# A decoder layer on one core: narrower merges, sample pieces scaled on ScalarE and spread over more of the program, early products in four banks, an operand read back from memory

## The chip, the cores and the metric

The kernel runs on one core of a Trainium2 chip. The metric is the device time of one execution in microseconds (us). Before the change three runs took 2405.36, 2413.23 and 2403.6 us; the median is 2405.36 us.

The core's engines, as the profile names them: PE multiplies matrices (PEld is its loading of weights), DVE is the vector engine (VectorE), ACT the scalar engine (ScalarE), POOL is GpSimd, which here mostly issues DMAs, SP issues the other DMAs. Each engine executes its own instructions strictly in the order in which they stand in the program; it waits at an instruction until what this needs is ready.

## What is computed

One inference step of one decoder layer, on 512 tokens of a prompt and 8 tokens that continue 8 samples with caches (T = 520 columns together):

```python
h = rmsnorm(x, ln_mix_pre)
aq, ak, av, bq, bk, bv, bz, bb, ba = split(h @ w_in)
# mixer A: 8 heads, three (window, dilation) branches, merged by softmax denominators
parts = [dilated_branch(aq, kk, vv, wnd, dil, rel_bias) for wnd, dil in ((128, 1), (512, 4), (2048, 16))]
att = merge_branches(parts)
# mixer B: gated delta rule, per token, computed in chunks
#   S_t = a_t (I - b_t k_t k_t^T) S_{t-1} + b_t k_t v_t^T,   o_t = S_t^T q_t
dn_out, conv_new, S_new = delta_mixer(bq, bk, bv, bz, bb, ba, ...)
x = x + rmsnorm(concat(att, dn_out) @ w_out, ln_mix_post)
# channel mixer
up = causal_dwconv(rmsnorm(x, ln_ffn_pre) @ w_ffn_in)      # 2048 -> 2 x 5632
x = x + rmsnorm((gelu(gate) * val) @ w_ffn_out, ln_ffn_post)
```

For a sample, attention reads 129 keys and values per branch from a cache in memory (8 samples x 2048 rows x 8 heads x 128), and the delta rule reads and rewrites a state of 8 samples x 8 heads x 128 x 128. The outputs are the new x for prompt and samples and the new caches and states.

## The kernel before

All large products are done in a split form: each fp32 operand is split into a high part (a cast on ACT) and a low part (a subtraction on DVE), and a product is three products, high x high, high x low and low x high. The 520 columns are handled as two halves, A and B, of 260.

**Units.** The input projection is 49 units, numbered idx 0 to 48. A unit is 128 output rows: 16 blocks of weights, three terms, two halves, 96 matmuls of 260 columns on PE (`gemm`, L148). Its weights come in pieces of 512 KB (`raw`, on SP's queue); `hi` is the cast (ACT, L117), `lo` the subtraction (DVE, L118), in five buffers of four blocks each. Each unit's end runs what depends on it. Units 25 to 40 make the keys and values of prompt attention and run the attention of a head when its second one is done (score maxima L883, transposed values L873 and L956, output copies `attm` L897); units 41 to 48 make the gate z. In between PE does the small matmuls of the delta rule.

**Merges.** The delta rule needs the inverse of a triangular 128 x 128 matrix per chunk and head. Blocks of 32 are inverted on DVE, written to memory (XD, XTD) and read back, and `merge(c)` (L525) joins them for each of four chunks c by small fp32 matmuls: five groups of eight (helper `four`, L520), each 128 weight columns by 128 moving columns, with masks m1 and m2 that keep the blocks that are meant. Its four-head results are `ym` tiles. Merges are emitted at idx 13, 14, 18 and 20.

**Sample work.** The work for the eight samples is one chain of Python generators, `samp`: 18 steps for the delta rule (`sample_dn`), 26 for the scores (`sample_scores`), 25 for the values (`sample_values`). Most steps use one piece `pc` of 512 KB (128 partitions x 8 x 128) of state, key cache or value cache, loaded on POOL's queue, four buffers, three pieces ahead (`ahead`). For a state piece, ACT scales eight blocks (L717), and DVE reduces them (L724) and adds the result (L726), twice. For a key piece DVE does eight product sums (L797). For a value piece DVE does eight scaled adds into `rows` (L833). From idx 25 on three steps are taken after each unit (`step(samp, 3)`), placed behind an instruction of that unit (`tc.issue_after`).

**Mid.** `mid A` and `mid B` are the output projection for the halves: 16 m, each 48 matmuls; ACT evicts each m twice (sqm L1050 and xa or xb L1051). `mid A` also steps `samp`, if anything is left of it.

**Channel mixer.** It is computed by a scheme with seven products of half-size operands (A11, A12, A22 and sums S1 to S4), each product 24 matmuls (`product`, L1264) on weights `hl` (cast L1185, subtraction L1186, four buffers). For the first sixteen blocks (EARLY) the products of A11 and A12 are done ahead, in pairs of two blocks: A11 for both, then A12 added in the same two banks ba and bb, each evicted by ACT to `sp` (L1324) and written to PD. Beside them a generator `gb` works out the half B's operands, a step at a time: S1 to S4 need A11 and A12 whole, which `whole` (L1105) forms again from high and low part by DVE adds (L1109). Then come the main products and the down projection (L1470).

A scheduler places the instructions of each engine from dependencies, priorities (`HI`) and the `issue_after` marks; their order is then fixed.

Of the kernel before, what the change touches and what calls it, by code (L numbers as in the profile page):

```python
# [10 lines left out]
F32 = mybir.dt.float32  # L11
# [15 lines left out]
KT = 16  # L27
H = 8
# [14 lines left out]
def trunk(ctx, tc, I, O):  # L43
# [361 lines left out]
    def col_sums(c, o, keep):  # L405

        p = bank()
        for h in range(4):
            PE.transpose(p[:, h * 128:h * 128 + 128], qkc(o + h, c), ident)
        if keep:  # L410
            kn = Pd.tile([128, 4, 128], F32, name="ym", bufs=3)
            V.tensor_copy(kn.rearrange("p a b -> p (a b)"), p)
            B.dma_start(KND[c], kn)
        jk = Pd.tile([128, 128], F32, name="jk", bufs=2)
        for h in range(4):
            S.activation(jk, p[:, h * 128:h * 128 + 128], AF.Square, accum_out=ss2[:, o // 4, c, h:h + 1])
# [39 lines left out]
    def kk(c, o):  # L456
        p = bank()
        for h in range(4):
            PE.matmul(p[:, h * 128:h * 128 + 128], qkc(4 + h, c), qkc(o + h, c), start=True, stop=True)
        k = Pd.tile([128, 4, 128], F32, name="ym", bufs=3)  # L460
        for h in range(4):
            S.activation(k[:, h, :], p[:, h * 128:h * 128 + 128], AF.Identity, scale=rqk[:, 1, c, h:h + 1])
        return k
# [53 lines left out]
    def four(lhs, rhs, g):  # L517
        p = bank()
        for j in range(4):
            PE.matmul(p[:, j * 128:j * 128 + 128], lhs(4 * g + j), rhs(4 * g + j), start=True, stop=True)  # L520
        return fl(p)

    TT = {}

    def merge(c):  # L525
        N = b4()
        B.dma_start(N, ALD[:, c])
        Tn = b4()
        B.dma_start(Tn, XD[:, c])
        Tt = b4()  # L530
        B.dma_start(Tt, XTD[:, c])
        ym = []
        for g in range(2):
            p = four(lambda h: N[:, h], lambda h: Tn[:, h], g)
            y = Pd.tile([128, 4, 128], F32, name="ym", bufs=3)
            V.tensor_mul(y, p, m1)
            ym.append(y)
        for g in range(2):
            p = four(lambda h: Tt[:, h], lambda h: ym[g][:, h % 4], g)
            pt = four(lambda h: ym[g][:, h % 4], lambda h: Tt[:, h], g)  # L540
            V.tensor_add(Tn[:, 4 * g:4 * g + 4], Tn[:, 4 * g:4 * g + 4], p)
            V.tensor_add(Tt[:, 4 * g:4 * g + 4], Tt[:, 4 * g:4 * g + 4], pt)
        ym = []
        for g in range(2):
            p = four(lambda h: N[:, h], lambda h: Tn[:, h], g)
            y = Pd.tile([128, 4, 128], F32, name="ym", bufs=3)
            V.tensor_mul(y, p, m2)
            ym.append(y)
        for g in range(2):
            pt = four(lambda h: ym[g][:, h % 4], lambda h: Tt[:, h], g)  # L550
            V.tensor_add(Tt[:, 4 * g:4 * g + 4], Tt[:, 4 * g:4 * g + 4], pt)
        TT[c] = Tt

    def scan(c):
# [99 lines left out]
    def ahead(loads):  # L654

        q = []
        for n in range(len(loads)):
            while loads and len(q) <= PCA:
                q.append(loads.pop(0)())
            yield n, q.pop(0)  # L660
# [7 lines left out]
    def sample_dn():  # L668
# [46 lines left out]
        def scaled(dst, src, j, pc):  # L715
            for k in range(8):
                S.activation(dst[:, k], src(k), AF.Identity, scale=kqd[:, j, pc * 8 + k:pc * 8 + k + 1])  # L717

        for pc, sp in ahead([lambda pc=pc: state_piece(pc) for pc in range(8)]):
            for j in range(2):  # L720
                pr = Psm.tile([128, 8, 128], F32, name="prod", bufs=1)
                scaled(pr, lambda k: sp[:, k], j, pc)
                dst = tmp[:, j] if pc else part[:, j * 128:j * 128 + 128]
                V.tensor_reduce(dst, pr.rearrange("p k v -> p v k"), axis=AX.X, op=OP.add)  # L724
                if pc:
                    V.tensor_add(part[:, j * 128:j * 128 + 128], part[:, j * 128:j * 128 + 128], dst)  # L726
            yield
        p = bank("bankX")
        PE.matmul(p[:, 0:258], kon[:, K_PR:K_PR + 128], part, start=True, stop=True)
        na = Psm.tile([128, 2], F32, name="dna")  # L730
# [93 lines left out]
    def sample_values():  # L824
        sc, sbias, stat = SA["sc"], SA["sbias"], SA["stat"]
        rows = Psm.tile([128, H, 128], F32, name="qrep")
        for x, t in ahead([lambda br=br, i=i: cache_piece(I["cache_v"], br, i) for br in range(3) for i in range(8)]):
            for h in range(H):
                w = sc[:, h, x:x + 1]
                if x == 0:  # L830
                    V.tensor_scalar(rows[:, h], t[:, h], w, None, op0=OP.mult)
                else:
                    V.scalar_tensor_tensor(rows[:, h], t[:, h], w, rows[:, h], op0=OP.mult, op1=OP.add)  # L833
            yield
        acc = Psm.tile([128, H, 8], F32, name="sacc")
        p = bank("bankX")
        for h in range(H):
            PE.matmul(p[:, h * 8:h * 8 + 8], rows[:, h], sel8[:, h], start=True, stop=True)
        V.tensor_copy(acc, hb(p[:, 0:64]))
        while len(kvT) < H or len(kvT[H - 1]) < 2:  # L840
            yield

        rows_of(kns, O["s_win_k"])
        rows_of(vns, O["s_win_v"])
        mc, lc, t, e = (stat[:, j] for j in range(4))
        V.tensor_mul(t, qs, kns)
        p = over_partitions(t.rearrange("p a b -> p (a b)"))
        V.tensor_sub(t, sbias[:, :, 24:25].to_broadcast([128, H, 8]), hb(p[:, 0:64]))
        V.tensor_max(e, mc, t)
        V.tensor_sub(t, t, e)  # L850
        V.tensor_sub(e, mc, e)
        S.activation(stat[:, 2:4], stat[:, 2:4], AF.Exp)

        V.tensor_scalar(t, t, 16.0, None, op0=OP.mult)
        V.tensor_mul(acc, acc, e)
        V.tensor_mul(e, lc, e)
        V.tensor_add(e, e, t)
        V.tensor_mul(t, vns, t)
        V.tensor_add(acc, acc, t)
        V.reciprocal(e, e)  # L860
        V.tensor_mul(attm[:, :, 512:520], acc, e)
        yield
# [62 lines left out]
    def step(g, n):  # L925
        for _ in range(n):
            if next(g, "end") == "end":
                return
# [7 lines left out]
    for idx, m in enumerate(mt_order):  # L936
# [50 lines left out]
            inverse()  # L987
        if 10 <= idx < 10 + H:
            bias_rows(idx - 10)
        if idx == 13:  # L990
            merge(0)
        if idx == 14:
            merge(1)
        if idx == 16:
            sample_conv()
# [11 lines left out]
        if idx >= 25:  # L1007

            with tc.issue_after(ev.ins):
                step(samp, 3)  # L1010
    Prs.close()


# [14 lines left out]
                split(MX[k][part], attm[:, k, o:o + w] if k < 8 else vdn[:, k - 8, o:o + w], o, w)  # L1028

    X1D = dram.tile([128, KT, T], F32, name="X1D")  # L1030

    def mid(part, also):

# [25 lines left out]
    def mid2(part, acc, mxs, wk):  # L1059
# [29 lines left out]
        if part == "A":  # L1089
            for g in range(8):  # L1090
                h = scale(g)
                for j in range(2):
                    t = xsA.tile([128, 2, w], F32R, name="xa")
                    split(t, h[:, j], 0, w)
                    XC["A11" if g < 4 else "A12"][2 * (g % 4) + j] = t
                yield
            return
# [4 lines left out]
                split(t, src[:, j], 0, w)  # L1102
                XC[name][2 * i + j] = t

        def whole(name, i):  # L1105
            a = wk.tile([128, 2, w], F32, name="ah", bufs=2)
            for j in range(2):
                t = XC[name][2 * i + j].bitcast(F32)
                V.tensor_add(a[:, j], t[:, 0], t[:, 1])  # L1109
            return a  # L1110

        for i in range(4):
            h1, h2 = scale(i), scale(4 + i)
            put("A22", i, h2, xsB)
            s = wk.tile([128, 2, w], F32, name="sd", bufs=2)
            V.tensor_sub(s, h1, h2)
            yield
            a1, a2 = whole("A11", i), whole("A12", i)
            V.tensor_sub(h1, a1, h1)
            put("S3", i, h1, sxp)  # L1120
            put("S1", i, s, xsB)
            yield
            V.tensor_sub(s, s, a1)
            put("S2", i, s, sxp)
            V.tensor_add(a2, a2, s)
            put("S4", i, a2, sxp)
            yield
# [8 lines left out]

    XC = {n: [None] * 8 for n in ("A11", "A12", "A22", "S1", "S2", "S3", "S4")}
    mix_split("A", mxA)
    a_ = mid("A", lambda m, ev: step(samp, 2))
    run_all(samp)  # L1140
    Pls.close()
    Pmb = ExitStack()
# [172 lines left out]


    for f in range(0, EARLY, 2):
        pp = [fbank(("ba", "bb")[i]) for i in range(2)]
        for k, n in enumerate(("A11", "A12")):
            for i in range(2):  # L1320
                product(pp[i], XC[n], first=k == 0)
                with HI():
                    t = wk2.tile([128, NA], F32, name="sp", bufs=2)
                    S.copy(t, pp[i][:, :NA])  # L1324
                    Q.dma_start(PD[order[f + i]][:, k], t)
                step(gb, 1)
# [326 lines left out]
```

## Time and profile before

| | before |
|---|---|
| median of three runs | 2405.36 us |
| the profiled execution | 2409.24 us |
| its span | 2407.4 us |
| instructions | 47633 |
| DMA traffic | 560.40 MB, mean 233 GB/s |
| PE waits for bankP, bankT and bankS of attention (L895, L873, L880) | 9.3, 6.5 and 3.6 us |
| PE waits for bankX (L1264) behind v L1367 | 6.0 us |
| PE waits for XD (L520) | 5.8 us |
| PE waits for sp in bb (L1264) | 5.3 us |

How to read the rows. A row of the waits names the engine that stood still, what its instruction works on and its line, then behind the arrow the engine and line that ended the wait; then us in all, how often, the longest. A row of the timeline has the start in us from the span's start, the length, engine, line, operation, what is written and read, the shapes, a count of merged instructions, and in brackets the idle time before it and what ended it. In a matmul's shape the first pair is the weights (rows * columns), the second what moves (partitions x columns). An fp32 matmul of the merges stands in the trace as two records. Ends of matmuls overlap, so that the distance between starts is the price of one. A row of the windows has the stretch, its length, the busy time of PE, PEld, DVE, ACT and POOL with counts, the granted clock of PE as a share of full speed, the share of the DMA engines' time and GB/s.

### The profile page before, as it was taken

What the parts mean: (1) busy time and instruction counts of PE and PEld (TensorE: products, weight loads), DVE (VectorE), ACT (ScalarE), POOL (GpSimd) and SP (SyncE); (2) the same over time, 40 slices, a digit from 0 to 9 for tenths busy, and PEclk for the clock granted to TensorE, in tenths of its full rate; (3) what the DMA queues carried; (4) which work ended last, traced back from release to release, by engine and by line L of the source; (5) the groups of instructions that cost most, each with busy time, mean ns of one, the idle gap of its engine ahead of it and who ended that gap; (6) DMA issues with size and microseconds to landing.
All of it is one profiled execution on the core that took longest, in us unless ns stands there. A gap on an engine that the chain in (4) does not pass through costs nothing.

```text
span 2407.4 us, 47633 instructions
## 1 busy us (share of the span) xinstructions
PE 2330.9 (97%) x19046; PEld 2306.0 (96%) x19046; DVE 1743.2 (72%) x3351; ACT 1088.6 (45%) x2124; POOL 173.9 (7%) x275
## 2 busy tenths in 40 slices
PE   8999999998899999899999999999999999999996
PEld 7999999997899999899999999999999999999996
DVE  7789454675789566887888777777777777856348
ACT  6443144683334555553334444444444454533234
POOL 1310110211110000000000000000000000000000
PEclk9999999998999999999999999999999999999998
DMA  5685742558995578878998888888889887687434
GB/s 182 237 288 186 260 158 97 173 176 232 235 197 168 190 246 279 287 226 252 279 274 252 253 262 266 266 260 262 266 264 300 285 313 262 230 297 253 151 112 135
DMA packets 155613, 560.40 MB, mean 233 GB/s; under 512 B 23304, under 2 KB 54968, under 8 KB 153344
## 3 DMA queue, kind: packets, MB, share of 16 engines
q1 hardware_dynamic: 125520, 466.31, 57.8%
q0 software_dynamic: 29872, 91.06, 15.1%
q8 instruction: 149, 2.44, 0.4%
q14 instruction: 72, 0.59, 0.1%
HBM read 498.37 MB, written 195.68 MB: 288 GB/s over the span
## 4 chain that ended last, share of the span: by engine, by line
PE 80%; DVE 7%; DMA 6%; issue 3%; ACT 3%; POOL 1%; SPq 0%; POOLq 0%; DVEq 0%; ACTq 0%
PE ps L1470 21%; PE ps L148 19%; PE bc L1264 10%; PE ba L1264 9%; PE bb L1264 7%; PE bankX L1264 5%; PE bd L1264 5%; DMA pc<-in_cache_k_dram 2%; ACT prod L717 2%; DVE dtmp L724 1%; DVE lo L118 1%; DVE b L502 1%; PE bankX L520 1%; PE bankP L520 1%; DMA XTD<-b 1%
## 5 line engine op out<-in xcount | busy, mean ns | idle before, releaser
L1470 PE MATMUL ps<-xb,hl 128*128 128x260 f32 x2112 | 487.3, 284 | 2.5 <-DVE yacc L1477 2.4
L1470 PE MATMUL ps<-xa,hl 128*128 128x260 f32 x2112 | 485.6, 283 | 0.3 <-DVE yacc L1477 0.2
L148 PE MATMUL ps<-xb,hi 128*128 128x260 f32 x1792 | 462.1, 289 | 0.6 <-ACT hi L117 0.6
L148 PE MATMUL ps<-xa,hi 128*128 128x260 f32 x1792 | 462.1, 289 | 0.3 <-DVE cv L346 0.3
L1470 PEld LDWEIGHTS ps<-xb,hl 128*128 128x128 f32 x2112 | 385.5, 189 | 3.3 <-ACT hl L1185 1.9
L1470 PEld LDWEIGHTS ps<-xa,hl 128*128 128x128 f32 x2112 | 385.6, 189 | 1.2 <-issue 0.7
L148 PEld LDWEIGHTS ps<-xb,hi 128*128 128x128 f32 x1792 | 332.7, 191 | 5.4 <-issue 2.8
L148 PEld LDWEIGHTS ps<-xa,hi 128*128 128x128 f32 x1792 | 333.3, 191 | 3.7 <-issue 1.7
L117 ACT CAST hi<-raw 128x512 fp32r<-128x512 f32 x320 | 194.5, 619 | 280.5 <-PE ps L148 240.8
L118 DVE TENSOR_TENSOR lo<-raw,hi 128x512 fp32r<-128x512 f32 x320 | 217.8, 688 | 116.4 <-ACT hi L117 115.3
L148 PE MATMUL ps<-xb,lo 128*128 128x260 f32 x896 | 258.4, 288 | 1.9 <-DVE lo L118 1.9
L148 PE MATMUL ps<-xa,lo 128*128 128x260 f32 x896 | 257.4, 287 | 0.2 <-DVE lo L118 0.2
L1264 PE MATMUL ba<-xa,hl 128*128 128x260 f32 x1728 | 221.0, 284 | 2.3 <-ACT hl L1185 2.3
L1264 PEld LDWEIGHTS ba<-xa,hl 128*128 128x128 f32 x1728 | 214.0, 190 | 2.4 <-ACT hl L1185 2.4
L1185 ACT CAST hl<-rw 128x1024 fp32r<-128x1024 f32 x131 | 137.6, 1051 | 167.7 <-PE ps L1470 53.9
L1186 DVE TENSOR_TENSOR hl<-rw,hl 128x1024 fp32r<-128x1024 f32 x131 | 160.2, 1223 | 69.0 <-ACT hl L1185 68.0
L1186 DVE TENSOR_TENSOR hl<-rx,hl 128x1024 fp32r<-128x1024 f32 x115 | 140.6, 1223 | 58.3 <-ACT hl L1185 57.9
L148 PEld LDWEIGHTS ps<-xb,lo 128*128 128x128 f32 x896 | 170.3, 190 | 4.3 <-DVE lo L118 2.7
L1185 ACT CAST hl<-rx 128x1024 fp32r<-128x1024 f32 x115 | 120.9, 1052 | 116.2 <-PE ps L1470 68.8
L148 PEld LDWEIGHTS ps<-xa,lo 128*128 128x128 f32 x896 | 170.8, 191 | 1.6 <-issue 0.7
L1185 ACT CAST hl<-rz 128x1024 fp32r<-128x1024 f32 x93 | 97.8, 1052 | 151.3 <-DVE rz L1223 51.3
L1186 DVE TENSOR_TENSOR hl<-rz,hl 128x1024 fp32r<-128x1024 f32 x93 | 113.8, 1224 | 64.2 <-ACT hl L1185 63.7
(579 smaller groups left out, 4193.0 us busy)
## 6 DMA issues: line engine op xcount, KB each, us to landing
raw<-in_w_in_dram SPq DMA_DIRECT2D x98, 512.0 KB, 4.8
raw<-in_w_out_dram SPq DMA_DIRECT2D x64, 512.0 KB, 4.2
rx<-in_w_ffn_in_dram SPq DMA_DIRECT2D x55, 512.0 KB, 6.9
rw<-in_w_ffn_in_dram SPq DMA_DIRECT2D x55, 512.0 KB, 6.1
ry<-in_w_ffn_in_dram SPq DMA_DIRECT2D x49, 512.0 KB, 4.4
rz<-in_w_ffn_in_dram SPq DMA_DIRECT2D x49, 512.0 KB, 6.2
rw<-in_w_ffn_in_dram POOLq DMA_DIRECT2D x44, 512.0 KB, 5.6
UD<-U SPq DMA_DIRECT2D x36, 522.0 KB, 7.2
```

Of the source, the lines that this page charges most:

```text
L117: S.copy(hi, r)
L118: V.tensor_sub(lo, r, hi.bitcast(F32))
L148: PE.matmul(ps[:, PO + o:PO + o + w_], w, X[k][part][:, b, :], start=(i == 0 and j == 0), stop=(i == n - 1 and j == 2))
L502: V.tensor_mul(v, Lb[:, None, 0:i, i].to_broadcast([128, i, i]), X[:, 0:i, 0:i].rearrange("p j m -> p m j"))
L520: PE.matmul(p[:, j * 128:j * 128 + 128], lhs(4 * g + j), rhs(4 * g + j), start=True, stop=True)
L717: S.activation(dst[:, k], src(k), AF.Identity, scale=kqd[:, j, pc * 8 + k:pc * 8 + k + 1])
L724: V.tensor_reduce(dst, pr.rearrange("p k v -> p v k"), axis=AX.X, op=OP.add)
L1185: S.copy(t[:, 0], raw)
L1186: V.tensor_sub(t[:, 1], raw, t[:, 0].bitcast(F32))
L1264: PE.matmul(p[:, 0:NA], w[:, a, k, :], X[k][:, c, :], start=first and n == 0, stop=n == 23, skip_group_check=not first)
L1470: PE.matmul(ps[:, PO + o_:PO + o_ + w_], t[:, a, i * 4 + k, :], act[4 * p + k][part][:, b, :], start=n == 0, stop=n == last)
```

## The change

1. Merges. The products move 64 columns instead of 128: only those halves of the blocks that the masks keep. Where the result has rows that are not needed, the weights are cut to 96 or 64 columns. The middle result of the first half lies in two new tiles YZ of 96 columns, zeroed once at the start. `ym` has two buffers instead of three. Merges of chunks 0 and 1 are emitted a unit later.
2. State pieces. The reduction over eight blocks is replaced by two adds of 512 elements per partition into `sums`, and one reduction at the end for each j.
3. Value pieces. The eight scaled adds on DVE become eight scalings in place on ACT (L848 of the new kernel) and one DVE add of 1024 elements per partition.
4. Two steps of `samp` after each unit instead of three; so 48 of the 69 are taken in the units and the rest in mid A, there two after each m, placed behind the eviction (`after(ev, samp, 2)`).
5. A11 and A12 are written to memory (HD) in fp32 when they are made, 8 tiles of 260 KB, and `whole` reads them back instead of adding the parts.
6. The early products of a pair use banks ba and bb or bc and bd in turn.

```diff
+    YZ = [Pd.tile([128, 4, 96], F32, name="yz", bufs=2) for g in range(2)]
+    for t in YZ:
+        G.memset(t, 0.0)
+
     def merge(c):
...
+        def half(lhs, rhs, g, w, M=128):
+            p = bank()[:M, 0:256].rearrange("p (a b n) -> p a b n", a=4, n=w)
+            for j in range(4):
+                PE.matmul(p[:, j], lhs(4 * g + j), rhs(4 * g + j), start=True, stop=True)
+            return p
...
+        for g in range(2):
+            p = half(lambda h: N[:, h], lambda h: left(Tn)[:, h], g, 32)
+            V.tensor_mul(yl(YZ[g]), p, left(m1))
+        for g in range(2):
+            p = half(lambda h: Tt[:, h], lambda h: yl(YZ[g])[:, h % 4], g, 32)
+            pt = half(lambda h: YZ[g][:, h % 4], lambda h: right(Tt)[:, h], g, 32, 96)
+            V.tensor_add(left(Tn[:, 4 * g:4 * g + 4]), left(Tn[:, 4 * g:4 * g + 4]), p)
+            V.tensor_add(right(Tt[:96, 4 * g:4 * g + 4]), right(Tt[:96, 4 * g:4 * g + 4]), pt)
...
         for pc, sp in ahead([lambda pc=pc: state_piece(pc) for pc in range(8)]):
             for j in range(2):
                 pr = Psm.tile([128, 8, 128], F32, name="prod", bufs=1)
                 scaled(pr, lambda k: sp[:, k], j, pc)
-                dst = tmp[:, j] if pc else part[:, j * 128:j * 128 + 128]
-                V.tensor_reduce(dst, pr.rearrange("p k v -> p v k"), axis=AX.X, op=OP.add)
                 if pc:
-                    V.tensor_add(part[:, j * 128:j * 128 + 128], part[:, j * 128:j * 128 + 128], dst)
+                    V.tensor_add(pr[:, 0:4], pr[:, 0:4], pr[:, 4:8])
+                    V.tensor_add(sums[:, j], sums[:, j], pr[:, 0:4])
+                else:
+                    V.tensor_add(sums[:, j], pr[:, 0:4], pr[:, 4:8])
             yield
+        for j in range(2):
+            V.tensor_reduce(part[:, j * 128:j * 128 + 128], sums[:, j].rearrange("p k v -> p v k"), axis=AX.X, op=OP.add)
...
         for x, t in ahead([lambda br=br, i=i: cache_piece(I["cache_v"], br, i) for br in range(3) for i in range(8)]):
             for h in range(H):
-                w = sc[:, h, x:x + 1]
-                if x == 0:
-                    V.tensor_scalar(rows[:, h], t[:, h], w, None, op0=OP.mult)
-                else:
-                    V.scalar_tensor_tensor(rows[:, h], t[:, h], w, rows[:, h], op0=OP.mult, op1=OP.add)
+                S.activation((t if x else rows)[:, h], t[:, h], AF.Identity, scale=sc[:, h, x:x + 1])
+            if x:
+                V.tensor_add(rows, rows, t)
             yield
...
-        if idx == 13:
+        if idx == 14:
             merge(0)
-        if idx == 14:
+        if idx == 15:
             merge(1)
...
             with tc.issue_after(ev.ins):
-                step(samp, 3)
+                step(samp, 2)
...
             for g in range(8):
                 h = scale(g)
+                Q.dma_start(HD[:, 2 * g:2 * g + 2], h)
...
-        def whole(name, i):
+        def whole(g):
             a = wk.tile([128, 2, w], F32, name="ah", bufs=2)
-            for j in range(2):
-                t = XC[name][2 * i + j].bitcast(F32)
-                V.tensor_add(a[:, j], t[:, 0], t[:, 1])
+            Q.dma_start(a, HD[:, 2 * g:2 * g + 2])
             return a
...
         for i in range(4):
+            a1, a2 = whole(i), whole(4 + i)
             h1, h2 = scale(i), scale(4 + i)
...
-            a1, a2 = whole("A11", i), whole("A12", i)
...
-    a_ = mid("A", lambda m, ev: step(samp, 2))
+    a_ = mid("A", lambda m, ev: after(ev, samp, 2))
...
-        pp = [fbank(("ba", "bb")[i]) for i in range(2)]
+        pp = [fbank((("ba", "bb"), ("bc", "bd"))[f // 2 % 2][i]) for i in range(2)]
```

More of the change, by code (lines that the diff above doesn't have):

```diff
@@ L410, in col_sums @@
         if keep:
-            kn = Pd.tile([128, 4, 128], F32, name="ym", bufs=3)
+            kn = Pd.tile([128, 4, 128], F32, name="ym", bufs=2)
             V.tensor_copy(kn.rearrange("p a b -> p (a b)"), p)
@@ L459, in kk @@
             PE.matmul(p[:, h * 128:h * 128 + 128], qkc(4 + h, c), qkc(o + h, c), start=True, stop=True)
-        k = Pd.tile([128, 4, 128], F32, name="ym", bufs=3)
+        k = Pd.tile([128, 4, 128], F32, name="ym", bufs=2)
         for h in range(4):
@@ L531, in merge @@
         B.dma_start(Tt, XTD[:, c])
+        def half(lhs, rhs, g, w, M=128):
[3 more added lines that the diff above has]
+            return p
+        v = lambda t, w: t.rearrange("p a (b n) -> p a b n", n=w)
+        left, right = (lambda t: v(t, 64)[:, :, :, 0:32]), (lambda t: v(t, 64)[:, :, :, 32:64])
+        yl = lambda t: v(t, 32)[:, :, 0:3:2]
@@ L532, in merge @@
         ym = []
         for g in range(2):
-            p = four(lambda h: N[:, h], lambda h: Tn[:, h], g)
-            y = Pd.tile([128, 4, 128], F32, name="ym", bufs=3)
-            V.tensor_mul(y, p, m1)
+            p = half(lambda h: N[:, h], lambda h: Tn[:, h, None, 0:64], g, 64)
+            y = Pd.tile([128, 4, 128], F32, name="ym", bufs=2)
+            V.tensor_mul(y[:, :, None, 0:64], p, m2[:, :, None, 0:64])
             ym.append(y)
         for g in range(2):
-            p = four(lambda h: Tt[:, h], lambda h: ym[g][:, h % 4], g)
@@ L540, in merge @@
[L540 to L551, printed above, removed]
+            pt = half(lambda h: ym[g][:, h % 4, 0:64], lambda h: Tt[:, h, None, 64:128], g, 64, 64)
@@ L552, in merge @@
+            V.tensor_add(Tt[:64, 4 * g:4 * g + 4, None, 64:128], Tt[:64, 4 * g:4 * g + 4, None, 64:128], pt)
         TT[c] = Tt
@@ L717, in scaled @@
                 S.activation(dst[:, k], src(k), AF.Identity, scale=kqd[:, j, pc * 8 + k:pc * 8 + k + 1])
+        sums = Psm.tile([128, H, 128], F32, name="qrep").rearrange("p (a b) v -> p a b v", a=2)
         for pc, sp in ahead([lambda pc=pc: state_piece(pc) for pc in range(8)]):
@@ L1030, in trunk @@
     X1D = dram.tile([128, KT, T], F32, name="X1D")
+    HD = dram.tile([128, KT, NA], F32, name="HD")
     def mid(part, also):
```

## Prediction

> **What bounds the kernel now.** I read the page first, for the engine that carries the time, then the waits of that engine, then the stretches in which those waits lie.
>
> ```profile
> PE 2330.9 (97%) x19046; PEld 2306.0 (96%) x19046; DVE 1743.2 (72%) x3351; ACT 1088.6 (45%) x2124; POOL 173.9 (7%) x275
> ...
> PE 80%; DVE 7%; DMA 6%; issue 3%; ACT 3%; POOL 1%; SPq 0%; POOLq 0%; DVEq 0%; ACTq 0%
> ```
>
> PE is busy 97% of the span and holds 80% of the chain that ended last. So the kernel gets faster only by fewer or shorter matmuls, or by PE waiting less; work taken from DVE or ACT is worth something only where PE waits for it. Who PE waited for, in us, times, longest:
>
> ```profile
> PE bankP L895 <- DVE attm L897: 9.3, 4, 6.6
> ...
> PE bankT L873 <- DVE vT L956: 6.5, 2, 4.2
> PE bankX L1264 <- DVE v L1367: 6.0, 1, 6.0
> PE bankS L520 <- DMA b<-XD: 5.8, 1, 5.8
> PE bb L1264 <- ACT sp L1324: 5.3, 3, 1.9
> PE bankS L880 <- DVE m L883: 3.6, 2, 3.4
> ```
>
> Three of the six (bankP L895, bankT L873, bankS L880) are one story: prompt attention waits for a DVE that stands elsewhere. The stretches show where, and two later ones beside them (columns: length, busy PE, PEld, DVE, ACT, POOL, granted clock, DMA share, GB/s):
>
> ```profile
> 560.00:580.00 20.00, 11.40 (x71) 11.04 (x70) 10.88 (x61) 4.48 (x9) 3.31 (x6) 0.73 0.74 200
> 580.00:600.00 20.00, 17.73 (x120) 17.02 (x119) 11.85 (x88) 4.44 (x11) 3.13 (x6) 0.85 1.05 229
> 600.00:620.00 20.00, 16.63 (x122) 15.39 (x122) 14.24 (x103) 7.21 (x16) 3.47 (x6) 0.91 0.92 201
> 620.00:640.00 20.00, 15.81 (x115) 15.17 (x115) 15.93 (x122) 4.92 (x12) 3.20 (x6) 0.91 0.94 283
> ...
> 980.00:1000.00 20.00, 14.68 (x115) 14.06 (x115) 15.06 (x18) 10.28 (x18) 0.00 (x0) 0.98 1.02 344
> ...
> 1020.00:1040.00 20.00, 20.00 (x170) 20.00 (x169) 20.00 (x39) 13.68 (x30) 0.00 (x0) 1.00 0.69 211
> ```
>
> From 560 to 640 PE loses 8.6+2.3+3.4+4.2 = 18.4 us of 80 idle, and works at a lower clock besides. These 80 us are the one large hole in the kernel.
>
> **The change part by part.** I sum against the profiled execution, 2409.24 us; the median of the runs, 2405.36, is 3.9 us below it, and I take those 3.9 off at the end.
>
> *Narrow merges.* Each of four merges has five groups of eight products, each product two records on PE: 80 records. All now move 64 columns, not 128. What a record costs is in these PE rows (start, length, line, shapes); weights are the first shape, moving columns the second:
>
> ```profile
> 271.34 0.42 PE L148 MATMUL ps<-xa,lo 128*128 128x260 f32 x1
> 271.56 0.42 PE L148 MATMUL ps<-xb,lo 128*128 128x260 f32 x1
> ...
> 273.01 0.28 PE L148 MATMUL ps<-xb,hi 128*128 128x260 f32 x1
> 273.12 0.28 PE L148 MATMUL ps<-xa,lo 128*128 128x260 f32 x1
> ...
> 273.73 1.05 PE L520 MATMUL bankP<-ym,b 128*128 128x128 f32 x8
> 274.62 1.06 PE L520 MATMUL bankX<-b,ym 128*128 128x128 f32 x8
> ...
> 754.36 0.51 PE L838 MATMUL bankX<-kon,qrep 128*128 128x8 f32 x4
> 754.72 0.36 PE L148 MATMUL ps<-xa,lo 128*128 128x260 f32 x1
> ...
> 961.36 0.60 PE L182 MATMUL bankT<-ones,acc 128*65 128x1 f32 x8 [1.09 <-DVE acc L1055]
> ```
>
> Eight records with 128 moving columns take 274.62 − 273.73 = 0.89 us, 0.111 each. Four with 8 moving columns take 754.72 − 754.36 = 0.36 us, 0.09 each, although they move a sixteenth. Eight with 65 weight columns and one moving column take 0.60 us in all, at most 0.075 each. So a small record follows its weight columns, not its moving ones. Of the 80 new records 48 keep 128 weight columns and save nothing to 0.02 us each; I take nothing, since the 0.09 includes a change from another shape. Sixteen have 96 weight columns and sixteen 64: scaled from 0.111, 0.083 and 0.056, a saving of 16 × 0.028 + 16 × 0.055 = 1.3 us for a merge, **5 us** for four (bounds 0 and, with 0.02 on the 48 as well, 9).
>
> The Trainium skill, "TensorE: Matmul & The Clock Gate", section "Back-to-back issue gap", gives an isolated matmul a gap that grows with its moving columns (N/2.4 + 2.5 ns). By that rule all 320 records would about halve; the row with 8 moving columns disagrees, and it decides.
>
> Emitting two merges one unit later does not touch PE's 5.8 us for XD. The first merge products stand in the same unit as before and wait for the same chain, inverse, write, read; I cost it at nothing. The first row of the change in PE's order (weight columns x moving columns):
>
> ```order
> L148 MATMUL ps<-xa,hi 128x260
> L542 MATMUL bankS<-b_2717,b_2715 128x64 x4
> L542 MATMUL bankT<-b_2717,b_2715 128x64 x4
> L148 MATMUL ps<-xb,hi 128x260
> L148 MATMUL ps<-xa,hi 128x260
> ```
>
> What moved here is only the second number, 128 to 64.
>
> *Two steps per unit.* The hole is the score stage of the samples. DVE needs the cache pieces pc there, and stands in order, with attention's copies behind (tile rows: first and last start at the end):
>
> ```profile
> DVE sjk L797 <- DMA pc<-in_cache_k_dram: 32.2, 12, 9.5
> ...
> L897 DVE COPY attm<-bankP x32: 275/284/295, 435.1 to 696.2; 128x128 f32<-128x128 f32 x32
> ...
> L797 DVE CUSTOM_DVE_ANT_0 sjk<-pc,qrep x192: 269/286/294, 564.1 to 651.4; 128x128 f32<-128x128 f32 x192
> ...
> L779 POOL DMA_DIRECT2D pc<-in_cache_k_dram x16: 578/578/612, 556.5 to 616.4; - x16
> ```
>
> The first piece comes late (a wait of 9.5 us), and 24 pieces then pass in 651.4 − 564.1 = 87 us, 3.7 each: that is the supply. The 32 attm copies belong to eight heads of two units, so a unit with its attention lasts about 261/15 = 17 us. At three pieces a unit the demand is 5.8 us a piece, and a lag of 10 us is made up at 2.1 a piece, over five pieces and more with each new delay. At two a unit the demand is 8.7, and the lag is gone after two. So the first stall stays (6.6 us, the longest for attm) and the others go.
>
> A stall costs more than itself: after the 5.8 us for XD matmuls start 0.22 us apart (271.34, 271.56), two microseconds later 0.11 to 0.12 (273.01, 273.12). In the four stretches the missing clock is 20 × (0.27+0.15+0.09+0.09) = 12 us, part of it in idle time where it costs nothing; I take 9. The hole is then 18.4 + 9 = 27 us, its first stall 6.6 + 2.4 = 9, the gain **18 us** (bounds 10, if two more stalls stay, and 22).
>
> The Trainium skill, same page, section "What's actually happening", lowers the clock after an idle window of about 3.4 us. By that rule the shorter stalls would cost only themselves and the gain would be about 14; the stretch 580:600, idle for 2.3 us in all, shows 0.85, so the trace does not agree.
>
> *Values on ScalarE, in mid A.* With two steps a unit 48 of 69 are done at the end of the units. Four value pieces fall in the last two units and twenty in mid A, two for each of its first ten m. What stands on ACT there (start, length, idle and releaser):
>
> ```profile
> 780.56 0.38 ACT L1050 ACTIVATE sqm<-ps 128x260 f32<-128x260 f32 x1
> 780.84 0.47 ACT L1051 ACTIVATE xa<-ps,cols 128x260 f32<-128x260 f32 x1
> 781.31 0.62 ACT L117 CAST hi<-raw 128x512 fp32r<-128x512 f32 x1
> 783.83 0.62 ACT L117 CAST hi<-raw 128x512 fp32r<-128x512 f32 x1 [1.90 <-PE ps L148]
> 785.27 1.14 ACT L117 CAST hi<-raw 128x512 fp32r<-128x512 f32 x2 [0.82 <-PE ps L148]
> 786.31 0.38 ACT L1050 ACTIVATE sqm<-ps 128x260 f32<-128x260 f32 x1
> ...
> 451.45 2.46 ACT L717 ACTIVATE prod<-pc,dkqd 128x128 f32<-128x128 f32 x8 [1.60 <-DVE dpart L724]
> ```
>
> One m lasts 786.31 − 780.56 = 5.75 us on PE, and ACT works 0.75 for sqm and xa plus four casts at 0.52: 2.85 us. The new operations are those of L717, eight in 2.36 (451.45 to the next at 453.81), 0.295 each; sixteen are 4.7 us. ACT's order in mid A, before (sqm and xa evict one m, hi are the weights of a later one):
>
> ```order
> L117 CAST hi<-raw 128x512 x2
> L1050 ACTIVATE sqm<-ps 128x260
> L1051 ACTIVATE xa<-ps,cols 128x260
> L117 CAST hi<-raw 128x512 x4
> L1050 ACTIVATE sqm<-ps 128x260
> ```
>
> and now:
>
> ```order
> L117 CAST hi<-raw 128x512 x3
> L1068 ACTIVATE sqm<-ps 128x260
> L1069 ACTIVATE xa<-ps,cols 128x260
> L848 ACTIVATE pc<-pc,sc 128x128 x16
> L117 CAST hi<-raw 128x512 x4
> L1068 ACTIVATE sqm<-ps 128x260
> ```
>
> The sixteen stand ahead of the casts that feed PE. 2.85 + 4.7 = 7.55 us against 5.75: ACT becomes the bound for ten m, 75.5 against 57.5 us. Casts run about one m ahead, which hides some 3.5 us: 14.5 us lost.
>
> The pieces must arrive too. In the value stage of before pieces (q0) and weights (q1) together fill the DMA engines from 695 to 715:
>
> ```profile
> DMA packets 1591, 3.96 MB, mean 198 GB/s; under 512 B 629, under 2 KB 629, under 8 KB 1590
> ...
> q0 software_dynamic: 1116, 2.21, 58.6%
> q1 hardware_dynamic: 474, 1.72, 45.8%
> ```
>
> One m needs 1.05 MB of pieces and 1.05 MB of weights, at 198 GB/s 10.6 us. That holds for the first sixteen pieces (two branches); of them seven are used or loaded when mid A begins, and nine are left, 48 us at 5.3 each, while ACT alone would want the ninth 41 us in (five m and half a sixth). So 6.5 us more, 21 in all; I take **20 us** (bounds 14, if transfers keep up, and 40, below). On DVE one add per piece replaces eight operations; DVE is not waited for there, so nothing.
>
> *State pieces by halves.* Shorter DVE work in a stage where PE hardly waits: nothing. *Early products.* PE waits 5.3 us for sp in bb. Four banks remove that, with the clock behind it up to 7 us. But PE's order, before:
>
> ```order
> L1264 MATMUL bb<-xa,hl 128x260 x7
> L190 MATMUL bankP<-nr_y,ones 128x65 x4
> L1264 MATMUL bb<-xa,hl 128x260 x17
> L1264 MATMUL ba<-xa,hl 128x260 x24
> L1264 MATMUL bb<-xa,hl 128x260 x24
> ```
>
> and now:
>
> ```order
> L1281 MATMUL bc<-xa,hl 128x260 x24
> L1281 MATMUL bd<-xa,hl 128x260 x8
> L1281 MATMUL ba<-xa,hl 128x260 x11
> L190 MATMUL bankP<-nr_y,ones 128x65 x4
> L1281 MATMUL ba<-xa,hl 128x260 x13
> L1281 MATMUL bb<-xa,hl 128x260 x24
> L1281 MATMUL bd<-xa,hl 128x260 x16
> ```
>
> starts products of the next pair early and leaves them open. Each holds its hl buffer (four) until its 24 are done, so casts and, behind them on ACT, evictions wait in turn. I take **3 us** gained (bounds 7 gained, 5 lost).
>
> *Operand read back.* Sixteen adds go from DVE, 8 × 260 KB are written and read on SP:
>
> ```profile
> L1109 DVE TENSOR_TENSOR ah<-xa 128x260 f32<-128x260 f32 x16 | 6.0, 424 | 0.0
> ```
>
> DVE is full from 1020 to 1040 yet PE loses nothing there, so the adds were covered; 4.2 MB more cost 0 to 6 us if the 980 to 1000 stretch (share 1.02) lasted for all of it. On SP the reads stand between weight loads, which they hold up if their buffer is late. I take nothing.
>
> Sum: −5 − 18 + 20 − 3 = −6; 2409.2 − 6 = 2403, less 3.9: **2399 us**. The uncovered 6.0 us before L1367 stay, as nothing there changes.
>
> **The rivals.**
>
> (1) ACT has more slack than I gave it and the four banks work: mid A costs 14, early products gain 7. −5 − 18 + 14 − 7 = −16, 2389 us. For it: the 1.90 and 0.82 us that ACT waits for PE in each m; against: the 198 GB/s above.
>
> (2) Slower: the transfers of mid A are the bound. By the share of the rows above one m takes 0.586 × 20 × 1.05/2.21 = 5.6 us of all engines for its pieces and 0.458 × 20 × 1.05/1.72 = 5.6 for its weights, 11.2. If no piece is ahead when mid A starts, six m at 11.2 and four at 7.55 take 97 instead of 57.5, +40. −5 − 18 + 40 − 3 = +14, 2419 us. It turns the whole slower from a loss of 26 us in mid A. For it: the share over 1 at 695 to 715; against: the first seven pieces come in units that last twice an m.
>
> (3) The score stage keeps its stalls, gain 10: −5 − 10 + 20 − 3 = +2, 2407 us. For it: the late first piece is untouched.
>
> (4) Merges pay by moving columns: 320 × 0.111/2 = 18 instead of 5, 2386 us. Against: the row at 754.36. (This is the rule of the Trainium skill's page on TensorE, above.)
>
> **How the numbers follow.** Chances: the forecast 0.42 (2392 to 2407), (1) 0.30, (2) 0.15, (3) 0.07, (4) 0.06. A measurement of this kernel tells about 0.5%, 12 us, from no change: 2393 and 2417. Faster: (4) 0.06, 0.24 of (1), 0.07 of the forecast's low end, 0.37. Slower: 0.12 of (2), 0.02 of the others' high ends, 0.14. The rest, 0.49, is the same. For 8 in 10 the range goes from 2380, which holds (1) and (4) with the bounds of the merges, to 2420, where most of (2) is left out.
>
> **What would show it.** In the profile after: records with 128 weight columns and 64 moving still 0.11 us apart; one PE stall of some 6 us at the first score piece and then none; in mid A an m of 7.5 to 10.6 us, PE idle for hi with ACT busy or waiting for pc; no wait for sp in bb, and some for hl. I am wrong if PE runs through mid A at 5.75 us an m, if the scores keep three or more stalls, or if new waits of over 5 us stand in the early products.

## The result

The changed kernel is slower: 2426.53 us (median of 4 runs, 2420.69 to 2429.43) against 2405.3, ratio 1.0074, 95% interval 1.0058 to 1.0089 (the ratios on record are not quite those of the medians). The forecast was 2399 and the range ended at 2420. The profiled execution has a span of 2427.6 us against 2407.4, 20.2 us more. The time of before differs by a few us from chip to chip (medians 2405 to 2411), so each ratio is taken against the runs of before that were made beside it.

PE does the same work and waits elsewhere. From the page of the changed kernel:

```profile
PE 2335.4 (96%) x19046; PEld 2307.4 (95%) x19046; DVE 1695.0 (70%) x3168; ACT 1140.7 (47%) x2316; POOL 172.7 (7%) x277
...
raw<-in_w_out_dram SPq DMA_DIRECT2D x64, 512.0 KB, 5.6
```

The last row, of the page of before:

```profile
raw<-in_w_out_dram SPq DMA_DIRECT2D x64, 512.0 KB, 4.2
```

Whom PE waited for in the changed kernel:

```profile
PE ps L148 <- ACT hi L117: 15.7, 11, 2.6
PE bankS L542 <- DMA b<-XD: 8.8, 1, 8.8
...
PE ps L148 <- DVE lo L118: 7.9, 12, 0.9
PE bankP L912 <- DVE attm L914: 7.4, 1, 7.4
...
PE ps L148 <- ACT mxA L168: 3.2, 1, 3.2
```

The waits for attention's copies fell from 9.3 + 6.5 + 3.6 us to one of 7.4 (and one of 1.5 for vT); waits for hi, lo and mxA, which were 0.6, 2.1 and 0.4 us, came in. Where that is: I number the large matmuls (260 columns) in PE's order, which both kernels execute in equal number, and subtract the start of the n-th in before from its start in the other trace. Negative is ahead of before. The first unit has 64 of them, so the units end at n = 4672 and mid A at 5440, where the lag is as at 5376; an m is 48. Each lag comes from one trace.

| up to here | n | changed kernel, us | in this part |
|---|---|---|---|
| delta rule with its merges done | 2592 | +1.5 | +1.5 |
| before the first scores | 3456 | −1.2 | −2.7 |
| scores and values of the units | 4512 | −19.2 | −18.0 |
| entry into mid A and mid A | 5376 | +18.6 | +37.8 |
| mid B | 6048 | +17.7 | −0.9 |
| early products | 6912 | +17.1 | −0.6 |
| all the rest | 17823 | +20.2 | +3.1 |

Two parts carry the result. The score stage gained what was forecast; that it is so to the microsecond is luck, as four of the runs below, whose edits only come behind this part, gained 15.6 to 17.3. The same four stretches as in the prediction, now:

```profile
560.00:580.00 20.00, 12.59 (x92) 12.41 (x91) 6.48 (x33) 4.48 (x10) 2.37 (x4) 0.83 0.84 232
580.00:600.00 20.00, 18.43 (x142) 17.11 (x141) 12.98 (x80) 8.68 (x21) 2.91 (x5) 1.00 1.02 232
600.00:620.00 20.00, 20.00 (x170) 19.95 (x169) 13.21 (x82) 6.48 (x14) 2.04 (x4) 1.00 0.79 201
620.00:640.00 20.00, 20.00 (x163) 19.25 (x162) 10.25 (x50) 7.77 (x17) 1.42 (x3) 1.00 0.74 165
```

One stall of 7.4 us is left in the first stretch and one of 1.5 in the second; from 600 on PE is full at full clock. Mid A took it all back, and as much again. ACT there (start, length; idle and what ended it in brackets):

```profile
776.13 0.62 ACT L117 CAST hi<-raw 128x512 fp32r<-128x512 f32 x1 [2.97 <-DMA raw<-in_w_out_dram]
776.65 0.38 ACT L1068 ACTIVATE sqm<-ps 128x260 f32<-128x260 f32 x1
776.93 0.47 ACT L1069 ACTIVATE xa<-ps,cols 128x260 f32<-128x260 f32 x1
777.29 4.79 ACT L848 ACTIVATE pc<-pc,sc 128x128 f32<-128x128 f32 x16
781.97 1.65 ACT L117 CAST hi<-raw 128x512 fp32r<-128x512 f32 x3
787.39 0.62 ACT L117 CAST hi<-raw 128x512 fp32r<-128x512 f32 x1 [3.76 <-DMA raw<-in_w_out_dram]
787.92 0.38 ACT L1068 ACTIVATE sqm<-ps 128x260 f32<-128x260 f32 x1
```

The sixteen scalings stand ahead of the casts and take 4.7 us (777.29 to 781.97), as forecast. But this m lasts 787.92 − 776.65 = 11.3 us instead of 7.55, and what ACT waits for is not a value piece, it is a weight (raw). In the whole of mid A ACT waits for no piece and 10.5 us for weights, and the median weight of the output projection lands 5.6 us after its issue instead of 4.2.

### The profile page after: what moved, and what is told of

It is laid out like the page before. It is cut to its first block, busy times and chain, and to the rows that moved or that the text cites. A ratio compares the mean times of both kernels' runs of the same rounds, so it can differ in the third digit from the quotient of the medians.

```text
span 2427.6 us, 47672 instructions
## 1 busy us (share of the span) xinstructions
PE 2335.4 (96%) x19046; PEld 2307.4 (95%) x19046; DVE 1695.0 (70%) x3168; ACT 1140.7 (47%) x2316; POOL 172.7 (7%) x277
## 4 chain that ended last, share of the span: by engine, by line
PE 60%; DMA 3%; ACT 2%; DVE 2%; issue 1%; SPq 0%; DVEq 0%; ACTq 0%
PE ps L1487 20%; PE bc L1281 11%; PE ba L1281 8%; PE bd L1281 6%; PE bb L1281 6%; PE bankX L1281 5%; PE ps L148 4%; DMA raw<-in_w_out_dram 2%; ACT pc L848 1%; DVE lo L118 1%; ACT hi L117 0%; DVE hl L1203 0%; ACT hl L1202 0%; DMA xb<-ACT 0%; DVE yacc L1541 0%
## 5 line engine op out<-in xcount | busy, mean ns | idle before, releaser
L148 PE MATMUL ps<-xa,hi 128*128 128x260 f32 x1792 | 468.1, 292 | 14.6 <-ACT hi L117 14.3
L1281 PE MATMUL ba<-xa,hl 128*128 128x260 f32 x1536 | 198.7, 286 | 4.4 <-ACT hl L1202 2.3
L1281 PEld LDWEIGHTS ba<-xa,hl 128*128 128x128 f32 x1536 | 191.7, 191 | 5.1 <-ACT sp L1341 2.5
```

The lines of the kernel that those rows point to most:

```text
L148: PE.matmul(ps[:, PO + o:PO + o + w_], w, X[k][part][:, b, :], start=(i == 0 and j == 0), stop=(i == n - 1 and j == 2))
L1281: PE.matmul(p[:, 0:NA], w[:, a, k, :], X[k][:, c, :], start=first and n == 0, stop=n == 23, skip_group_check=not first)
```

## The experiments

The theories: ACT, whose scalings hold up the casts; the transfers, which make weights late; ACT's order alone, with late weights as its consequence. The first two runs take one away each. Lags are those of the table above: mid A is the change of the lag from n = 4512 to 5376.

**The scalings without the loads.**

```diff
-        for x, t in ahead([lambda br=br, i=i: cache_piece(I["cache_v"], br, i) for br in range(3) for i in range(8)]):
+        for x, t in ahead([lambda br=br, i=i: kept(br, i) for br in range(3) for i in range(8)]):
```

(`kept` loads the first eight pieces and then hands out the last four tiles again.)

> The changed kernel, but value pieces 9 to 24 are not loaded: the scalings of mid A and the adds stay and work on the four tiles that pieces 5 to 8 left (so the values of the samples are wrong). ACT's order in mid A stays. In the trace of the changed kernel the stretch from the last units to the end of mid A's sample work loses 38 us against before. Theory 1, ACT is the bound (scalings ahead of the casts, 7.55 us an m): the loss falls to 15, about 2404 us. Theory 2, it is the transfers, and the scalings alone would be hidden by casts that run ahead: the loss falls to 5 or less, about 2392 us. Theory 3, ACT's order does all of it and late weights only follow from it: the loss stays over 30, about 2425 us.

Measured: 2414.54 us in one run, mid A −18.5 to +4.2, a loss of 22.7: no theory's number, above the 15 of the first and below the 30 of the third, while the second, with 5, falls. Between the starts of successive sqm, nine m in a row last 7.4 to 7.6 us, which is the prediction's 7.55 for an m bound by ACT.

**The loads without the scalings.**

```diff
-            for h in range(H):
+            for h in range(H) if x < 4 else ():
                 S.activation((t if x else rows)[:, h], t[:, h], AF.Identity, scale=sc[:, h, x:x + 1])
```

> The changed kernel, but only the first four value pieces are scaled on ACT: the other twenty are loaded and added as they are (so the values of the samples are wrong), and no scaling stands on ACT in mid A. Theory 1 (ACT's 7.55 us an m and late loads add up): the loss of 38 us falls to about 15 to 20, about 2407 us. Theory 2 (transfers): it stays at 30 or more, about 2422 us or over. Theory 3 (ACT's order alone): it falls to 5 or less, about 2392 us.

Measured: 2417.92 us in one run, mid A −15.2 to +6.0, a loss of 21.2. The third theory falls: with no scaling on ACT the weights are late all the same. Mid A from 740 to 860 in before, in the changed kernel, in the run without loads and in the run without scalings (one fence each; the same columns as above), and ACT's wait for weights in that stretch, which before does not have:

```profile
740.00:860.00 120.00, 117.39 (x946) 115.79 (x946) 78.86 (x175) 62.42 (x134) 1.74 (x3) 0.97 0.51 167
```

```profile
740.00:860.00 120.00, 94.87 (x642) 90.20 (x641) 71.49 (x110) 92.00 (x265) 11.83 (x21) 0.86 0.78 202
...
ACT hi L117 <- DMA raw<-in_w_out_dram: 10.5, 6, 3.8
```

```profile
740.00:860.00 120.00, 102.82 (x764) 97.69 (x763) 82.21 (x137) 101.99 (x292) 2.90 (x5) 0.94 0.52 154
...
ACT hi L117 <- DMA raw<-in_w_out_dram: 1.3, 1, 1.3
```

```profile
740.00:860.00 120.00, 103.60 (x776) 100.11 (x775) 83.54 (x143) 59.31 (x138) 11.83 (x21) 0.93 0.83 228
...
ACT hi L117 <- DMA raw<-in_w_out_dram: 32.2, 10, 5.4
```

Without the loads ACT is busy 102 of 120 us and weights are in time but for 1.3 us. Without the scalings ACT is half idle, waits 32.2 us for weights, and PE, busy 103.6 us, is no better off than without the loads (102.8). Either cause alone costs about the same, and together less than their sum, which leaves the question what both runs share.

**Neither.** The last two edits together; only the adds on DVE stay.

> The changed kernel with both taken away: pieces 9 to 24 not loaded and pieces 5 to 24 not scaled, only their adds on DVE stay (so the values of the samples are wrong). With the scalings alone mid A lost 23 us, with the transfers alone 21, with both 38. Theory, two separate causes that overlap: with neither the loss is under 5 us, about 2389 us. Rival, a third cause common to all three runs (the adds on DVE, or the entry into mid A): 10 us or more stay, 2397 us.

Measured: 2397.57 us in one run, mid A −18.7 to −9.8, a loss of 8.9. Between theory and rival, nearer to the rival. Of it 6.3 fall up to n = 4896, that is in the last unit and the first four to five m; I call this the entry. There PE waits, as in the changed kernel, 3.2 us for mxA, whose casts stand on ACT behind the gate of the last unit and the scalings of the units' last pieces, and 3.0 for a cast whose weight came late (the first eight pieces are still loaded in this run, and the first four scaled, so the entry is not free of either cause):

```profile
PE ps L148 <- ACT mxA L168: 3.2, 1, 3.2
PE ps L148 <- ACT hi L117: 3.0, 1, 3.0
PE ps L148 <- DVE mxA L169: 1.4, 2, 0.7
PE ps L148 <- DVE lo L118: 1.1, 2, 0.9
```

Behind the entry, and up to the end of the chain, an m lasts 5.8 us as before, so the adds on DVE, the rival's other cause, cost nothing there. So the 37.8 us are 8.9 for the entry and the rest, 13.8 more for the scalings alone (22.7 − 8.9), 12.3 more for the loads alone (21.2 − 8.9), and 2.8 for both at once. Each figure is a difference of single traces; the 15.6 to 17.3 above show how far such figures scatter, so the 2.8 is not told from nothing.

**Values on DVE, same place.**

```diff
-                S.activation((t if x else rows)[:, h], t[:, h], AF.Identity, scale=sc[:, h, x:x + 1])
-            if x:
-                V.tensor_add(rows, rows, t)
+                w = sc[:, h, x:x + 1]
+                if x == 0:
+                    V.tensor_scalar(rows[:, h], t[:, h], w, None, op0=OP.mult)
+                else:
+                    V.scalar_tensor_tensor(rows[:, h], t[:, h], w, rows[:, h], op0=OP.mult, op1=OP.add)
```

> The changed kernel with the value pieces scaled and added on DVE as before (sixteen operations of 0.29 us in an m, beside four subtractions at 0.58: about 7.1 us a m of 5.75), still two a m in mid A. Theory, the place is at fault: mid A loses about as much as with ACT, 30 to 38 us, 2419 to 2427 us. Rival, the move to ACT is at fault (casts kept back by scalings): ACT's casts run free, only late weights stay, loss 21 us as with no scaling, about 2410 us or less.

Measured: 2417.75 us in one run; mid A −19.3 to +12.1, a loss of 31.4. The place is at fault; with the move to ACT it is some 6 us more.

**Three steps a unit.**

```diff
-                step(samp, 2)
+                step(samp, 3)
```

> The changed kernel with three steps after each unit again, so that all 69 are done before mid A. All theories: mid A at 5.75 us an m, its 38 us gone. Theory of the prediction on the scores: their 18 us of stalls come back, 2426 - 38 + 18 = 2406 us, ratio to before 1.000. Rival: two steps a unit had no part in the gain at the scores, 2388 us. Second rival: three scalings of a value piece in each z unit (7.1 us of ACT beside 4.2 of casts in 11.5) cost something of their own, 2410 to 2416 us.

Measured: 2398.45 against 2411.11 us, ratio 0.9945 (0.9929 to 0.9961). Mid A loses nothing (lag −7.6 to −7.9), as all theories said, and no cost appears in the z units. But the scores kept 7.9 us of the gain (lag +0.3 at n = 3456, −7.6 at 4512), which no theory had. This is the lowest ratio of the study and under both kernels; its interval overlaps that of the next run.

**State pieces alone,** the second edit of the change on the kernel before (its diff is above, in the section on the change).

> The kernel before with the state pieces added by halves and nothing else. In the run with three steps after each unit the score stage lost about 8 us less than in the kernel before, although its demand for pieces was the same; only the state stage in front of it had changed. Theory: shorter DVE work in the state stage (4.6 to 2.8 us a step) lets the last state pieces be written and the first key pieces be loaded earlier, so that this alone gains about 8 us, ratio 0.996 to 0.997. Rival (the prediction): nothing, 1.000.

Measured: 2401.26 against 2410.4 us, ratio 0.9963 (0.9951 to 0.9975). The lag is −3.0 at n = 3456 and −10.9 at 4512: 7.9 us at the scores, the same as in the last run, and 3 ahead of them. DVE's wait for key pieces, in this run:

```profile
DVE sjk L801 <- DMA pc<-in_cache_k_dram: 21.3, 11, 4.5
```

Before it was 32.2 us with a first wait of 9.5. DVE around the first score, before and in this run:

```profile
564.11 0.29 DVE L797 CUSTOM_DVE_ANT_0 sjk<-pc,qrep 128x128 f32<-128x128 f32 x1 [9.49 <-DMA pc<-in_cache_k_dram]
...
565.81 1.28 DVE L753 SCALAR_TENSOR_TENSOR pc<-pc,dsac,prod 128x1024 f32<-128x1024 f32 x1
...
569.83 0.28 DVE L897 COPY attm<-bankP 128x128 f32<-128x128 f32 x1
```

```profile
561.18 1.29 DVE L757 SCALAR_TENSOR_TENSOR pc<-pc,dsac,prod 128x1024 f32<-128x1024 f32 x1 [3.90 <-DMA pc<-in_state_rec_dram]
562.38 0.28 DVE L901 COPY attm<-bankP 128x128 f32<-128x128 f32 x1
567.14 0.29 DVE L801 CUSTOM_DVE_ANT_0 sjk<-pc,qrep 128x128 f32<-128x128 f32 x1 [4.47 <-DMA pc<-in_cache_k_dram]
```

With shorter adds the scheduler places the last state piece (L753, now L757) and attention's copy ahead of the first score, where the first score stood ahead of both, and what stands behind it is held up less. That this order is the whole of the 7.9 us was not tested by itself.

**Merges alone,** the first edit on the kernel before.

> The kernel before with the narrow merges alone (with their ym in two buffers and two merges a unit later). In the trace of the changed kernel the stage of the delta rule stood 1.5 us behind before when it ended. Theory now: the merges gain about as much as the lost ym buffer and the longer wait for XD cost, ratio 0.999 to 1.001. Rival, the 5 us of the prediction: 0.998. Rival, records paid by moving columns, 18 us: 0.9925.

Measured: 2407.95 against 2411.11 us, ratio 0.9987 (0.9974 to 1.0001): not told from no change, and the 5 us of the prediction lie inside too. The trace is clearer (PE rows of this run):

```profile
268.79 1.94 PE L542 MATMUL bankS<-b,b 128*128 128x64 f32 x8 [8.44 <-DMA b<-XD]
...
277.83 0.84 PE L542 MATMUL bankX<-b,yz 128*96 128x64 f32 x8
278.51 1.06 PE L542 MATMUL bankS<-yz,b 128*128 128x64 f32 x8
279.41 0.84 PE L542 MATMUL bankT<-b,yz 128*96 128x64 f32 x8
...
284.19 0.68 PE L542 MATMUL bankS<-b,ym 128*64 128x64 f32 x8
284.80 1.11 PE L542 MATMUL bankP<-b,b 128*128 128x64 f32 x8
```

Eight records of 128 weight columns and 64 moving take 279.41 − 278.51 = 0.90 us, 0.112 each, as with 128 moving; with 96 weight columns 278.51 − 277.83 = 0.68, 0.085 each; with 64, 0.61, 0.076, which has the step to the next group's 128 in it: the median distance between neighbours within such groups of this trace is 0.058. So the records cost what was forecast. What was not: the wait for XD is 8.4 instead of 5.8 us. PE reaches it at 260.35 instead of 261.61, and resumes at 268.79 instead of 267.36: the read lands at 268.65 instead of 267.22. This is no accident of one execution: over all traces the wait is 4.8 to 6.0 us in the four with the old merges and 7.6 to 11.0 in the ten with the new ones. In all ten the last block of XTD is also issued later on POOL, at 246.6 to 250.9 us instead of 242.1 to 243.3. Which part of the edit delays the chain, the place of the merges or their buffers, was not tested.

**Early products and read back alone,** edits 5 and 6 on the kernel before.

> The kernel before with the operand read back and the early products in four banks, and nothing else. In the traces so far the stage of the early products ended where it had begun, against before (-0.6 to +1.2 us). Theory: the waits for sp go and new ones come, 0, ratio 0.9995 to 1.0005. Rival, the 3 us of the prediction: 0.9988. Second rival, the reads hold up the weights behind them on SP: 1.001 or more.

Measured: 2415.11 against 2409.26 us, ratio 1.0024 (1.0013 to 1.0035), slower. That is the second rival's number; its reason is not shown. In its trace +2.8 us are there at n = 4416, at the scores, where this edit changed nothing; the stage of the early products itself goes from +3.5 to +5.5. Of the 6 us in the trace 2 belong to the edit's place; where the rest comes from was not pursued.

**Fewer pieces for mid A.** Nine are left for it by

```diff
-                step(samp, 2)
+                step(samp, 2 if 31 <= idx < 44 else 3)
```

with two steps an m as in the change, and then with one (`after(ev, samp, 1)`).

> The changed kernel with three steps after units 25 to 30 and 44 to 48 and two between, so that nine value pieces instead of twenty are left for mid A, two a m for about five m, eight of them from the third branch whose packets are large. Theory, ACT at 7.55 us an m and late weights: five m at 7.5 to 8.5, loss 9 to 14 us against 38, about 2399 us. Rival, the loss is the entry into mid A and not its rate: over 25 us, 2413 us.

> The same with one step after each m of mid A: 2.85 + 2.4 = 5.2 us of ACT in an m of 5.75, 0.5 MB of pieces beside 1 MB of weights. Theory, the rate of ACT and of the transfers decides: mid A loses 0 to 4 us and the scores keep most of their gain, 2385 to 2393 us, ratio 0.990 to 0.993. Rival, any scaling ahead of the casts costs (2.4 us an m, a lead that is used up): nine m, 15 us or more, ratio 0.997.

Measured: with two 2409.59 us in one run, mid A −20.6 to −3.8, 16.8 us, over the theory's 14 and well under the rival's 25. With one 2408.07 against 2410.4 us, ratio 0.9995 (0.9986 to 1.0004), mid A −19.6 to −4.3, 15.3 us: the rival's number, though not its reason. More than half, 8.3, is lost in the last unit and the first m (−19.6 to −11.3 at n = 4704), 7.0 behind it with ACT at 5.2 us an m. PE's waits from 740 to 860:

```profile
PE ps L148 <- ACT hi L117: 4.7, 2, 4.1
PE ps L148 <- DVE lo L118: 3.8, 6, 2.0
PE ps L148 <- ACT mxA L168: 3.4, 1, 3.4
PE ps L148 <- DVE mxA L169: 1.6, 2, 0.9
```

**Two steps at the start of the scores only** (`2 if 31 <= idx < 35 else 3`), on the changed kernel and on the kernel with the state pieces alone. One step without a piece is left for mid A.

> The changed kernel with two steps only after units 31 to 34, the first of the score stage, and three after all others, so that one step without a piece is left for mid A. Theory: the stalls at the scores come from the late first piece, and two steps while the lag is made up are enough; the scores keep 14 to 19 of 19 us, mid A and its entry lose nothing, 2388 to 2396 us, ratio 0.990 to 0.994. Rival: three steps a unit stall again as soon as they return, no better than three throughout, 0.9945.

> The kernel before with the state pieces added by halves and two steps after units 31 to 34, nothing else (values on DVE, merges and early products as before). Theory: the same gain as the last, since the other parts of the change bring nothing, ratio 0.990 to 0.994. Rival: values on DVE beside the units' subtractions keep DVE full, and part of the gain is lost there, 0.996.

Measured: ratio 0.9978 (0.9964 to 0.9993) and 0.9976 (0.9967 to 0.9985). The scores gain 8.4 and 6.9 us (−1.8 to −10.2, −4.3 to −11.2, both at n = 4320): the rival, stalls return with the third step. The longest, for vT, is 8.9 and 9.6 us and comes at n = 3739, after the third step is back; the changed kernel has no stall there. And both lose 9.1 and 7.5 us by the end of mid A, although no piece is left for it, while three steps throughout and the state pieces alone lose nothing. On the kernel with the state pieces alone nearly all of the 7.5 is one wait of PE itself, at the product of the chain that follows the last value piece (L842, L838 of before), which stands in PE's order inside the first m of mid A, while DVE is still adding the last values:

```profile
PE bankX L842 <- DVE qrep L837: 6.4, 1, 6.4
```

On the changed kernel the loss is spread: from 715 to 800 us PE waits 3.1 us for lo, 2.4 for the gate (kT), 2.2 at this product and 1.2 for hi. So a chain that runs late at the entry can cost there with no piece left to step; on the kernel with the state pieces alone the way is seen, on the changed kernel it is not told apart.

## Why the prediction was wrong, point by point

*Mid A, +20 forecast, +37.8 measured: this term failed.* Its part for ACT, 14.5, was right (13.8 by the runs). The part for the transfers, 6.5, was built on the wrong wait: "the pieces must arrive too". ACT waited for no piece in mid A; POOL issues them well ahead. What came late is the other stream, the weights on SP, with three buffers and no lead to give when a load lands 8 to 15 us after its issue. That cost 12.3 us alone, and at most 2.8 more together with ACT. And the entry, not costed at all, took most of the 8.9 that stay with neither. Rival (2) had the price, +40, by the share of the packets' time, and the wrong condition: it wanted the pieces to be missing. It had a chance of 0.15.

*Scores, −18 forecast, −18.0 measured,* with one stall of 7.4 us where 6.6 were forecast to stay. The number is right by luck, since the cause was only half mine: the state pieces alone bring 7.9 of it, and two steps instead of three, which were to bring all, the other 10 or so.

*State pieces by halves, "nothing".* Wrong: ratio 0.9963, the best single edit. I looked for waits of PE in the state stage and found hardly any; the stage sets when the next one starts and, through the scheduler, in which order.

*Merges, −5.* The records cost what the weight columns said: 0.112, 0.085 and 0.058 within groups where 0.111, 0.083 and 0.056 were used. The gap of an isolated matmul by moving columns (the Trainium skill, "TensorE: Matmul & The Clock Gate", "Back-to-back issue gap") does not describe them, since 64 columns cost what 128 did. But "does not touch PE's 5.8 us for XD" failed: the wait grew to 8.8 (8.4 alone), and the lag after the stage is +1.5 instead of −5.

*Early products and read back, −3.* "Four banks remove that" failed: the waits for sp moved to three banks and hardly fell, from 5.3 us to 2.1 + 1.9 + 1.0, and were 4.0 + 1.9 + 0.5 with the two edits alone. The stage won 0.6 in the changed kernel and lost 2.0 with the edits alone, inside the bounds; that run as a whole lost more, ratio 1.0024.

*The 6.0 us before L1367, "stay".* They fell to 1.9 in this execution, and to 3.9 with the merges alone: DVE waits for a transfer (sst) just ahead of v, 3.6 us before and 1.1 now, and this varies.

The sum: −6 forecast, +20.2 in the trace. Of the 26 between, 18 are mid A, 6.5 the merges, 2.4 the early products and 3 the rest, against 2.7 won in the state stage and 0.9 in mid B.

## What to carry to other kernels

Work that is moved into a stage must be priced on each of that stage's streams, also on the one that it does not feed: here the loads that came late were those of the stage's own weights. A stage in which PE does not wait can still hold the next stage's start, and a chain of work that is late where one stage hands over to the next can hold the next one up, in one run by a single product that stands in order among its first.

## What the runs showed of the hardware

With 64 moving columns an fp32 record keeps the price of its weight columns: 0.112 us for 128, 0.085 for 96, 0.058 for 64. A 512 KB weight of the output projection that landed 3.0 to 5.1 us after its issue in mid A of before, where no value pieces are loaded, took 7.8 to 14.6 us beside the value pieces of the first two branches, at some 200 GB/s in all. In mid A, where no wait of PE was longer than 3.2 us, the granted clock was 0.86 over 120 us. The Trainium skill (the same page, "What's actually happening") lowers it after an idle window of about 3.4 us; here shorter waits were enough. In before a single wait of 2.27 us, from 590.61 to 592.88, is followed by 3.42 us (592.92 to 596.34) at a granted clock of 0.50.
